# The block sums of G move from VectorE to GpSimd in a seven-product matrix multiplication

## The chip, the cores and the metric

The kernel runs on one core of a Trainium2 chip. The time is device microseconds of one execution; three runs of the kernel before are at hand. Five engines matter, each with its own instruction queue, executed in order: TensorE (PE in the profile, its weight loads PEld), VectorE (DVE), ScalarE (ACT), GpSimd (POOL) and the queue engine SP. Transfers between main memory and the on-chip memory (SBUF) are issued from a queue and carried by 16 DMA engines. TensorE writes to eight accumulator banks (PSUM).

## The reference

The kernel computes a weight gradient: the sum over all 16 x 512 = 8192 rows of the outer products of `input` (X, 1024 columns) and `grad_output` (G, 768 columns), in 32-bit floats.

```python
"input": np.random.randn(16, 512, 1024), "grad_output": np.random.randn(16, 512, 768)
grad_weight = np.einsum('bmk,bmn->kn', input, grad_output)   # 1024 x 768
```

## The kernel before, in words

**Tiles.** The 8192 rows are 32 units of 256 rows. A unit is one tile `xp` (128 partitions x 2 x 1024, bf16) and one tile `gp` (128 x 2 x 768, bf16); the transfer converts from 32 bits. `LOADS` names the kind of each unit: units 0 to 5 and 31 ("s") are multiplied in the ordinary way, units 6 to 30 ("P", 25 pairs) with seven block products in place of eight.

**The seven products.** For a pair, X and G are seen as 2 x 2 blocks: two halves of the rows by two halves of the columns (512 of X, 384 of G). `sum_x` forms three sums of blocks of X in three instructions, two of them into the tile `xe`, the last over a block of `xp` (stages x0, x1, x2); `sum_g` forms three of G into `ge` and, last, over a block of `gp` (stages g0, g1, g2). g0 adds two blocks at once (128 x 768), g1 adds a block to g0's result (128 x 384), g2 adds a block to g1's (128 x 384). The products are named by a letter or digit: A and 1 read raw blocks, B needs x2, C needs g2, 5 and 7 need x0 and g0, 6 needs x1 and g1 (`operands`, lines 224 to 243). Products are accumulated over many units, each in four strips of 128 columns of X (a name such as C2 is product C, strip 2).

**The plan.** The order on TensorE, VectorE and ScalarE is written out by hand in the list `PLAN`, and is executed as it stands. A token such as `C2.1` is one matmul of C2, `C2@2.2` is two into bank 2, newly opened; `fC3@6` fills bank 6 with an accumulated sum from SBUF (ScalarE), `v10` and `c10` close a bank into SBUF (VectorE or ScalarE), `x0.9` and `g2.9` are stages of the sums of unit 9. Around the last sum of G of pair 9 the plan reads:

```
60@6.3 cC1 61@2.1 g1.9 61.2 fB0@0 v60 10@5.2 c61 g2.9 B0.3 v10 fC3@6 C2@2.2 cB0 x0.9 C2.1
```

Sums come shortly before the products that read them: here `C2.1` is the first product to read g2 of pair 9. For pair 25 it is the first of `C2.3` in `50.4 vB2 B0@6.1 x0.25 f10@2 B0.3 c50 C2@5.1 x1.25 C2.3`.

**Transfers.** Unit 0's first half comes through SP and ScalarE. All other loads are issued by GpSimd, in order of the units, G ahead of X (lines 151 to 159): two issues for each unit from 2 on. An issue waits until the eighth issue before it has landed, that is, X of unit u+4 waits for X of unit u, and G of u+4 for G of u. Where a tile's buffer is used again (14 are held), it also waits for its last readers. Before the change nothing else stands on GpSimd's queue but four constants at the start. The results are stored by SP, the last also by ScalarE.

Of the kernel before, what the change touches and what calls it, by code (L numbers as in the profile page):

```python
# [9 lines left out]
P = 128  # L10

LOADS = "ssssssPPPPPPPPPPPPPPPPPPPPPPPPPs"
# [69 lines left out]
SUMS_HELD = 10  # L82

MERGED = 2


@with_exitstack
def kernel(
# [6 lines left out]
    nc = tc.nc  # L95
# [11 lines left out]
    X = input.rearrange("b m k -> (b m) k")  # L107
    G = grad_output.rearrange("b m n -> (b m) n")
# [35 lines left out]
    items = []  # L144
    tiles = {}
    for u, kind in enumerate(LOADS):
        pool = pairs if u else head
        xp = pool.tile([P, 2, K], bf16, name="xp", tag="xp")
        gp = pool.tile([P, 2, N], bf16, name="gp", tag="gp")
        if u >= MERGED:  # L150
            rows = slice(2 * u * P, 2 * (u + 1) * P)
            nc.gpsimd.dma_start(out=gp, in_=G[rows, :].rearrange("(p m) n -> p m n", m=2))  # L152
            nc.gpsimd.dma_start(out=xp, in_=X[rows, :].rearrange("(p m) k -> p m k", m=2))  # L153
        for h in range(2):
            s = 2 * u + h
            if s > 0 and u < MERGED:
                nc.gpsimd.dma_start(out=gp[:, h, :], in_=G[s * P : (s + 1) * P, :])
            if s > 1 and u < MERGED:
                nc.gpsimd.dma_start(out=xp[:, h, :], in_=X[s * P : (s + 1) * P, :])
            if kind == "s":  # L160
                items.append(("s", xp[:, h, :], gp[:, h, :]))
        tiles[u] = (xp, gp)
        if kind == "P":
            items.append(("P", u, None))

    extra = {}

    def sums_of(u):
        if u not in extra:
            extra[u] = (
                sums.tile([P, 3, KH], bf16, name="xe"),
                sums.tile([P, 3, NH], bf16, name="ge"),
            )
        return extra[u]
# [11 lines left out]
    def sum_g(stage, u):  # L189
        g = tiles[u][1].rearrange("p m (h n) -> p (m h) n", h=2)  # L190
        ge = sums_of(u)[1]
        if stage == 0:
            nc.vector.tensor_add(out=ge[:, 0:2, :], in0=g[:, 0:2, :], in1=g[:, 1::2, :])  # L193
        elif stage == 1:
            nc.vector.tensor_add(out=ge[:, 2, :], in0=g[:, 3, :], in1=ge[:, 0, :])  # L195
        else:
            nc.vector.tensor_add(out=g[:, 1, :], in0=ge[:, 2, :], in1=g[:, 2, :])  # L197

    def round_by(engine, dst, src, c0, c1):
        copy = nc.vector.tensor_copy if engine == "DVE" else nc.scalar.copy  # L200
# [129 lines left out]
    for token in PLAN:  # L330
        op, rest = token[0], token[1:]
        if op in "xg":
            stage, u = rest.split(".")
            (sum_x if op == "x" else sum_g)(int(stage), int(u))
        elif op == "r":
            round_by(*ROUNDINGS[int(rest)])
        elif op == "f":
            block, banks = rest.split("@")
            b, _, b2 = banks.partition("+")
            fill(block[0], int(block[1]), int(b), int(b2) if b2 else None)  # L340
        elif op in "cv":
            close(op, rest[0], int(rest[1]))
        else:
            block, n = token.split(".")
            block, _, b = block.partition("@")
            multiply(block[0], int(block[1]), int(b) if b else None, int(n))
# [32 lines left out]
```

## Time and profile before

| | |
|---|---|
| median of 3 runs | 162.96 us (162.92 to 163.28) |
| profiled execution, span from first to last instruction | 161.4 us; the median of the runs is 1.56 us longer |
| mean TensorE clock granted | 0.995 |
| matmuls | 937, from 0.8 to 157 us |
| VectorE busy | 143.0 us, of which sums of G 31.2, sums of X 38.0 |
| GpSimd busy | 34.6 us, nearly all of it 65 transfer issues |
| transfers from GpSimd | 60 of 384 or 512 KB, median 16.7 us from issue to landing |

The profile gives for the profiled execution only its span, no time of its own outside it. A row of a group reads: line, engine, operation, output <- inputs, shapes, count, then busy microseconds and mean nanoseconds of one, then the idle time of the engine just before. A row of the timeline reads: start, length, engine, line, operation, count. VectorE's and ScalarE's instructions overlap a little, so that the next starts some 0.08 us before the one before has ended.

### The profile page before, as it was taken

How to read it: one execution, taken by the hardware profiler on the slowest of the kernel's cores; microseconds unless marked ns; L12 is line 12 of the kernel's file. 1: busy time of each engine (PE TensorE's matmuls, PEld its weight loads, DVE VectorE, ACT ScalarE, POOL GpSimd, SP SyncE). 2: the span in 40 equal slices, each digit the busy share in tenths (PEclk: the TensorE clock that was granted, in tenths of full speed). 3: DMA queues.
4: the chain of work that ended last, by engine and by line, in shares of the span. 5: the costliest groups of instructions: out<-in, count | busy, mean ns of one | idle time of the engine just before them, and what ended most of it. 6: DMA issues, size and time to landing. Idle time of an engine off the chain costs nothing.

```text
span 161.4 us, 2771 instructions
## 1 busy us (share of the span) xinstructions
PE 156.2 (97%) x937; PEld 92.2 (57%) x937; DVE 143.0 (89%) x323; ACT 112.6 (70%) x253; POOL 34.6 (21%) x69
## 2 busy tenths in 40 slices
PE   8999999999999999999999999999999999999990
PEld 3355555666566665556665556665566665655560
DVE  0688986889999999999999998998899988989991
ACT  3679627749978999978878786525676278877630
POOL 7442221222221222222221222221222100000000
PEclk9999999999999999999999999999999999999998
DMA  5999999999999999999999999999999999905275
GB/s 168 297 211 213 211 216 212 212 214 211 215 211 215 213 211 213 213 212 214 210 214 214 216 213 213 211 212 211 212 212 213 213 213 213 202 18 195 107 283 195
DMA packets 12398, 33.40 MB, mean 207 GB/s; under 512 B 1376, under 2 KB 4192, under 8 KB 12384
## 3 DMA queue, kind: packets, MB, share of 16 engines
q0 software_dynamic: 9360, 28.64, 89.7%
q1 hardware_dynamic: 2592, 3.47, 6.2%
q10 hardware_dynamic: 432, 1.11, 1.9%
q8 instruction: 7, 0.11, 0.3%
q14 instruction: 7, 0.06, 0.1%
HBM read 58.72 MB, written 3.15 MB: 383 GB/s over the span
## 4 chain that ended last, share of the span: by engine, by line
PE 89%; DVE 4%; DMA 3%; issue 2%; ACT 1%; DVEq 0%; ACTq 0%
PE bank L286 89%; DMA xf<-in_input_dram 3%; DVE acc L310 2%; DVE macc L306 1%; DVEq L374 0%; DVE acc L325 0%; DVE macc L310 0%; DVE acc L323 0%; ACT bank L273 0%; ACT xp L201 0%; DVE macc L307 0%; DVEq L306 0%; ACTq L273 0%
## 5 line engine op out<-in xcount | busy, mean ns | idle before, releaser
L286 PE MATMUL bank<-gp,xp 128*128 128x384 bf16 (+2 forms) x631 | 110.2, 325 | 0.2
L286 PEld LDWEIGHTS <-xp 128*128 128x128 bf16 x631 | 61.4, 98 | 42.9 <-DVE xp L201 1.6
L286 PE MATMUL bank<-ge,xe 128*128 128x384 bf16 x300 | 56.2, 326 | 0.0
L273 ACT COPY bank<-macc 128x384 f32<-128x384 f32 x71 | 33.6, 484 | 13.0 <-DVE macc L325 5.5
L286 PEld LDWEIGHTS <-xe 128*128 128x128 bf16 x300 | 29.3, 98 | 19.5 <-issue 0.2
L273 ACT COPY bank<-acc 128x384 f32<-128x384 f32 (+1 forms) x70 | 32.3, 479 | 9.4 <-DVE acc L323 5.5
L321 ACT COPY macc<-bank 128x384 f32<-128x384 f32 x61 | 28.6, 479 | 9.4 <-PE bank L286 8.1
L325 DVE TENSOR_TENSOR acc<-bank,acc 128x384 f32<-128x384 f32 x54 | 28.7, 552 | 3.2 <-PE bank L286 1.6
L153 POOL DMA_DIRECT2D xp<-in_input_dram x30 | 15.9, 530 | 53.7 <-DMA xp<-in_input_dram 30.0
L321 ACT COPY acc<-bank 128x384 f32<-128x384 f32 x45 | 21.4, 480 | 7.3 <-PE bank L286 6.9
L152 POOL DMA_DIRECT2D gp<-in_grad_output_dram x30 | 15.9, 532 | 36.8 <-DMA gp<-in_grad_output_dram 14.4
L325 DVE TENSOR_TENSOR macc<-bank,macc 128x384 f32<-128x384 f32 x41 | 22.5, 551 | 0.5 <-PE bank L286 0.2
L183 DVE TENSOR_TENSOR xe<-xp 128x1024 bf16<-128x1024 bf16 x25 | 17.1, 682 | 0.3 <-DMA xp<-in_input_dram 0.3
L323 DVE COPY acc<-bank 128x384 f32<-128x384 f32 x24 | 13.1, 554 | 3.6 <-PE bank L286 3.0
L193 DVE TENSOR_TENSOR ge<-gp 128x768 bf16<-128x768 bf16 x25 | 13.7, 549 | 0.0
L187 DVE TENSOR_TENSOR xp<-xp,xe 128x512 bf16<-128x512 bf16 x25 | 10.5, 419 | 0.4
L185 DVE TENSOR_TENSOR xe<-xe,xp 128x512 bf16<-128x512 bf16 x25 | 10.4, 418 | 0.3
L197 DVE TENSOR_TENSOR gp<-ge,gp 128x384 bf16<-128x384 bf16 x25 | 8.8, 351 | 0.3
L195 DVE TENSOR_TENSOR ge<-gp,ge 128x384 bf16<-128x384 bf16 x25 | 8.7, 349 | 0.2
L310 DVE TENSOR_TENSOR acc<-bank,macc 128x384 f32<-128x384 f32 (+2 forms) x17 | 8.0, 523 | 0.0
L323 DVE COPY macc<-bank 128x384 f32<-128x384 f32 x14 | 7.6, 552 | 0.4 <-PE bank L286 0.4
L201 DVE CAST gp<-gf 128x192 bf16<-128x192 f32 (+1 forms) x2 | 0.7, 325 | 5.0 <-DMA gf<-in_grad_output_dram 5.0
(17 smaller groups left out, 22.2 us busy)
## 6 DMA issues: line engine op xcount, KB each, us to landing
xp<-in_input_dram POOLq DMA_DIRECT2D x30, 512.0 KB, 16.7
gp<-in_grad_output_dram POOLq DMA_DIRECT2D x30, 384.0 KB, 16.7
out_dram<-acc SPq DMA_DIRECT2D x15, 192.0 KB, 1.9
xf<-in_input_dram ACTq DMA_DIRECT2D x2, 512.0 KB, 5.0
gp<-in_grad_output_dram POOLq DMA_DIRECT2D x3, 192.0 KB, 6.7
xp<-in_input_dram POOLq DMA_DIRECT2D x2, 256.0 KB, 8.0
gf<-in_grad_output_dram SPq DMA_DIRECT2D x2, 192.0 KB, 4.2
out_dram<-acc SPq DMA_DIRECT2D x1, 128.0 KB, 2.0
```

Source lines behind the costliest of these rows:

```text
L152: nc.gpsimd.dma_start(out=gp, in_=G[rows, :].rearrange("(p m) n -> p m n", m=2))
L153: nc.gpsimd.dma_start(out=xp, in_=X[rows, :].rearrange("(p m) k -> p m k", m=2))
L183: nc.vector.tensor_sub(out=xe[:, 0:2, :], in0=x[:, 1::-1, :], in1=x[:, 3::-2, :])
L185: nc.vector.tensor_sub(out=xe[:, 2, :], in0=xe[:, 0, :], in1=x[:, 0, :])
L187: nc.vector.tensor_add(out=x[:, 1, :], in0=x[:, 2, :], in1=xe[:, 2, :])
L193: nc.vector.tensor_add(out=ge[:, 0:2, :], in0=g[:, 0:2, :], in1=g[:, 1::2, :])
L273: nc.scalar.copy(out=tile_[:, 0 : c1 - c0], in_=src[:, c0:c1])
L286: nc.tensor.matmul(tile_[:, 0 : c1 - c0], stat, mov[:, c0:c1], start=first and j == 0, stop=True, skip_group_check=True,)
L310: nc.vector.tensor_add(out=dst[:, c0:c1], in0=b, in1=sum_of(SHARED[p], q)[:, c0:c1])
L321: nc.scalar.copy(out=dst, in_=b)
L323: nc.vector.tensor_copy(out=dst, in_=b)
L325: nc.vector.tensor_add(out=dst, in0=b, in1=dst)
```

## The change

The three stages of `sum_g` are given to GpSimd, with the same operands. The loads are no longer all issued ahead of the plan: those up to unit 10 are (`AHEAD + LOADS.index("P")` is 10, the units 0 to 9, and stage 0 of unit 6 asks for unit 10), and from then on the loads of unit u+4 are issued right ahead of stage 0 of unit u. The plan itself isn't touched; its tokens `g0` to `g2` now stand on another queue.

In the changed program GpSimd's queue holds, for each pair u: the issue of G of unit u+4, the issue of X of unit u+4, g0, g1, g2 of unit u; g1 waits for g0 and g2 for g1 by a semaphore. The last four sums (27 to 30) have no issues between them. Ahead of the very first g0 stands one control instruction (`PseudoReloadLibraryIndex`, shown at line 203). VectorE has 75 instructions fewer.

```diff
@@ the loads @@
-        if u >= MERGED:
-            rows = slice(2 * u * P, 2 * (u + 1) * P)
-            nc.gpsimd.dma_start(out=gp, in_=G[rows, :].rearrange("(p m) n -> p m n", m=2))
-            nc.gpsimd.dma_start(out=xp, in_=X[rows, :].rearrange("(p m) k -> p m k", m=2))
...
+    issued = [0]
+
+    def issue_loads(upto):
+        while issued[0] < min(upto, len(LOADS)):
+            u = issued[0]
+            issued[0] += 1
+            xp, gp = tiles[u]
+            if u >= MERGED:
+                rows = slice(2 * u * P, 2 * (u + 1) * P)
+                nc.gpsimd.dma_start(out=gp, in_=G[rows, :].rearrange("(p m) n -> p m n", m=2))
+                nc.gpsimd.dma_start(out=xp, in_=X[rows, :].rearrange("(p m) k -> p m k", m=2))
+                continue
...
+    issue_loads(AHEAD + LOADS.index("P"))
@@ sum_g @@
         if stage == 0:
-            nc.vector.tensor_add(out=ge[:, 0:2, :], in0=g[:, 0:2, :], in1=g[:, 1::2, :])
+            issue_loads(u + 1 + AHEAD)
+            nc.gpsimd.tensor_add(out=ge[:, 0:2, :], in0=g[:, 0:2, :], in1=g[:, 1::2, :])
         elif stage == 1:
-            nc.vector.tensor_add(out=ge[:, 2, :], in0=g[:, 3, :], in1=ge[:, 0, :])
-        else:
-            nc.vector.tensor_add(out=g[:, 1, :], in0=ge[:, 2, :], in1=g[:, 2, :])
+            nc.gpsimd.tensor_add(out=ge[:, 2, :], in0=g[:, 3, :], in1=ge[:, 0, :])
+        else:
+            nc.gpsimd.tensor_add(out=g[:, 1, :], in0=ge[:, 2, :], in1=g[:, 2, :])
```

`AHEAD` is 4.

More of the change, by code (lines that the diff above doesn't have):

```diff
@@ L84 @@
 MERGED = 2
+AHEAD = 4
 @with_exitstack
@@ L149 @@
         gp = pool.tile([P, 2, N], bf16, name="gp", tag="gp")
-        if u >= MERGED:
-            rows = slice(2 * u * P, 2 * (u + 1) * P)
-            nc.gpsimd.dma_start(out=gp, in_=G[rows, :].rearrange("(p m) n -> p m n", m=2))
[L153 to L161, printed above, removed]
         tiles[u] = (xp, gp)
-        if kind == "P":
+        if kind == "s":
+            items += [("s", xp[:, h, :], gp[:, h, :]) for h in range(2)]
+        else:
             items.append(("P", u, None))
+    issued = [0]
[9 more added lines that the diff above has]
+                continue
+            for h in range(2):
+                at = slice((2 * u + h) * P, (2 * u + h + 1) * P)
+                if u or h:
+                    nc.gpsimd.dma_start(out=gp[:, h, :], in_=G[at, :])
+                if u:
+                    nc.gpsimd.dma_start(out=xp[:, h, :], in_=X[at, :])
+    issue_loads(AHEAD + LOADS.index("P"))
     extra = {}
```

## The prediction

> **What bounds the kernel now.** I read the page's busy times and slices first, then a window of the middle, the chain that ended last, the groups by line, and the timeline around single pairs.
>
> ```profile
> span 161.4 us, 2771 instructions
> PE 156.2 (97%) x937; PEld 92.2 (57%) x937; DVE 143.0 (89%) x323; ACT 112.6 (70%) x253; POOL 34.6 (21%) x69
> PEclk9999999999999999999999999999999999999998
> 20.00:140.00 120.00, 120.00 (x740) 72.22 (x739) 112.66 (x257) 87.93 (x199) 25.86 (x49) 1.00 1.07 213
> 17.61 132.31 PE bank L286 x812
> ```
>
> Lines four and five are a window (us, then busy PE, PEld, DVE, ACT, POOL, clock, DMA share, GB/s) and a piece of the chain. TensorE is busy 120.00 of 120 us at full clock, and the chain is matmuls alone from 17.6 to 149.9. So any time that a matmul waits in the middle is added to the end, and nothing taken off VectorE there can shorten it. POOL has time free: 25.86 of 120 us, all issues.
>
> ```profile
> L193 DVE TENSOR_TENSOR ge<-gp 128x768 bf16<-128x768 bf16 x25 | 13.7, 549 | 0.0
> L197 DVE TENSOR_TENSOR gp<-ge,gp 128x384 bf16<-128x384 bf16 x25 | 8.8, 351 | 0.3
> L195 DVE TENSOR_TENSOR ge<-gp,ge 128x384 bf16<-128x384 bf16 x25 | 8.7, 349 | 0.2
> L310 DVE TENSOR_TENSOR acc<-bank,macc 128x384 f32<-128x384 f32 x15 | 7.5, 547 | 0.0
> L310 DVE TENSOR_TENSOR acc<-bank,macc 128x128 f32<-128x128 f32 x1 | 0.3, 280 | 0.0
> L321 ACT COPY acc<-bank 128x384 f32<-128x384 f32 x45 | 21.4, 480 | 7.3 <-PE bank L286 6.9
> L273 ACT COPY bank<-acc 128x128 f32<-128x128 f32 x1 | 0.3, 263 | 0.0
> ```
>
> These are the prices: the three adds as they are now (0.55 + 0.35 + 0.35 = 1.25 us a pair), and two sizes each of a VectorE add and a ScalarE copy that take one element at a time, from which a rate follows.
>
> ```profile
> 34.83 0.53 POOL L153 DMA_DIRECT2D xp<-in_input_dram  x1 [1.92 <-DMA xp<-in_input_dram]
> 45.91 0.55 DVE L193 TENSOR_TENSOR ge<-gp 128x768 bf16<-128x768 bf16 x1
> 47.24 0.35 DVE L197 TENSOR_TENSOR gp<-ge,gp 128x384 bf16<-128x384 bf16 x1
> 46.94 3.25 PE L286 MATMUL bank<-gp,xp 128*128 128x384 bf16 x19
> 48.11 0.53 POOL L153 DMA_DIRECT2D xp<-in_input_dram  x1 [2.24 <-DVE macc L325]
> 115.74 0.36 DVE L197 TENSOR_TENSOR gp<-ge,gp 128x384 bf16<-128x384 bf16 x1
> 117.30 1.46 PE L286 MATMUL bank<-gp,xp 128*128 128x384 bf16 x8
> 117.08 0.53 POOL L153 DMA_DIRECT2D xp<-in_input_dram  x1 [1.88 <-DMA xp<-in_input_dram]
> ```
>
> The timeline (start, length). The issues of X for units 10, 13 and 29 stand at 34.83, 48.11 and 117.08. Each waits until the eighth issue before it has landed, here X of units 6, 9 and 25. From the first to the last are 19 pairs in 82.25 us: 4.33 us a pair is the transfers' pace. The last sum of pair 9 ends at 47.6. By the plan's order, after 1(0) x2, B0 x3 and C2 x2, the eighth matmul of the row at 46.94 is the first that reads it, at 46.94 + 7 x 0.1625 = 48.1 (20 us hold about 123 matmuls: 120.00 / 740). Pair 25's last sum ends at 116.1, and its reader, the sixth of the row at 117.30, starts at 118.1. The slack is 0.5 and 2.0 us.
>
> **The change, part by part.** The matmuls and their order stay; 75 adds go from VectorE's queue to POOL's.
>
> *Removed from VectorE:* 25 x 1.25 = 31 us of busy time. Worth 0: matmuls hide it, since none waits for an eviction in the middle (120.00 of 120). If sums come late, VectorE waits with TensorE and has this time to spare, so evictions add nothing either.
>
> *Place on POOL's queue:* the issues up to unit 10 come ahead of the first sum, in the order of before. From then on, the sums of pair u stand behind the issues of unit u+4, and the last of these waits for X of pair u to land, which the G sums themselves don't need. For pair 9: the issue starts at 48.11 and takes 0.53, so the adds start at 48.64, not at 45.91. Even at VectorE's speed they end at 49.9, where 48.1 is wanted: 1.8 us late.
>
> *The price of three adds on POOL* is shown by no row; POOL's only computing rows are constants one element wide (98 ns), which is a fixed part at most. Low end: VectorE's 1.25 us. For more: an engine that takes its two operands one after the other pays two passes. ScalarE's rate is (480 - 263) / 256 = 0.85 ns an element beside 0.155 us fixed; two passes over 768, 384 and 384 elements come to 1.46 + 0.81 + 0.81 = 3.07 us. VectorE's 32-bit rate, (547 - 280) / 256 = 1.04 ns beside 0.147, gives 3.65. High end: two passes at the slowest row, ScalarE's cast of 192 elements in 351 ns (1.83 ns each): 5.6 us. I take 3.4 us, between the two fitted rates, the rows nearest to an engine that streams. The Trainium skill, GPSIMD Engine Reference, Performance versus the Vector engine, has 4497 ns for an add of 2048 fp32 elements; scaled to 1536 that is an estimate of 3.4 us and would leave the sum where it is; no run here shows it yet.
>
> *POOL's period:* two issues of 0.53 and 3.4 make 4.46 us, above the transfers' 4.33. POOL becomes the slowest of the stages, and lateness grows by pair.
>
> *A control instruction* without a counterpart before stands ahead of the first add (line 203 of the changed kernel). No row has it: 0 at least; ScalarE's table load, 1.28 us, is the nearest of its kind and I take 1.3. It is paid once, and while POOL is the slowest, it stays in the end.
>
> *Added waits:* the second add waits for the first and the third for the second, now by POOL's semaphore (in the rate's uncertainty). Behind a waiting issue or add stand the next pair's issues. That starves no transfer: four pairs, 17 us of them, are under way, against at most some 5 us of adds. SP's and ScalarE's queues keep their order.
>
> *Contention:* VectorE keeps the three X sums of each pair, 0.68 + 0.42 + 0.42 = 1.52 us, which read two SBUF tensors as POOL's adds will. Whether the two engines can read at once is what no row shows: POOL reads no tile before, and X's first sum takes 679 to 691 ns whatever POOL issues. If not, they take turns, and POOL's period grows by what of the 1.52 does not fall under its 1.06 of issues: by 0.46 at least, 1.52 at most. So it is 4.92 to 5.98, middle 5.45. Nothing excludes that it is 0; I take the middle, since POOL would be reading 3.4 of 4.46 us, so a shared path would be met by nearly every X sum.
>
> *The sum:* the first add starts at 34.83 + 0.53 + 1.3 = 36.7. Pair 25's last add ends at 36.7 + 19 x 5.45 + 3.4 = 143.7, 25.6 us after 118.1. Pair 9's would be 8.4 late (36.7 + 3 x 5.45 + 3.4 = 56.5), so pair 25 decides. The span: 161.4 + 25.6 = 187.0. The runs' median is 162.96, 1.56 above the profiled span; the time is 188.6.
>
> The Trainium skill, SBUF — State Buffer, Who interferes with whom, says that a VectorE instruction with two SBUF inputs and a GpSimd instruction that reads SBUF exclude each other for a whole instruction. By that rule it is 188.6, and by the rows alone, where nothing slows down beside POOL, 169.7 (below). No trace here shows either yet.
>
> **Rivals.**
>
> *No turns.* Both engines read at once. Pair 25 ends at 36.7 + 19 x 4.46 + 3.4 = 124.8, 6.7 late: span 168.1, time 169.7. For it: no row shows interference. Against it: nothing in this trace either, the case doesn't occur. Its bounds are 166.6 (3.07 us: POOL keeps the transfers' pace, and pair 9 is late by 48.64 + 3.07 - 48.1 = 3.6) and 174.7 (3.65 us: 36.7 + 19 x 4.71 + 3.65 - 118.1 = 11.7).
>
> *Cheap adds.* POOL adds 16-bit data about as fast as VectorE. Then POOL keeps up, and only its place on the queue costs: 1.8 us at pair 9, some 2.3 with the control instruction, which delays the first pair. Time 164.8 to 165.3. Against it: POOL would have to add an element in 0.52 ns ((549 - 349) / 384, VectorE's 16-bit rate), against 0.85 to 1.04 for the engines above that take one element at a time, and without a second pass.
>
> *Not slower.* The sums of pair 9 come by 48.1 because the issue ahead of them lands its wait earlier. The trace gives X of pair 9 as landed by 48.0, since VectorE starts its first X sum at 48.01. It decides only if the adds run ahead of that issue, by 1.8 us at least. Then TensorE runs as before: 162.9, and at best some 0.6 less, the gaps between matmuls from 8.4 us on. Only a reordering of POOL's queue could bring it; the changed program's order shows the issue ahead.
>
> *The moves don't happen:* excluded, the changed program has 75 adds more on POOL and 75 fewer on VectorE.
>
> **How the numbers follow.** Turns: 0.50, 188.6, with 178.5 at 4.92 and 198.6 at 5.98 us a pair. No turns: 0.31, 169.7. Cheap adds: 0.15, 165. Not slower: 0.04. The range is 166 to 202: below it lie the not slower case and most of the cheap one; above it, adds of over 3.8 us with turns. The likeliest case alone: 177 to 202. Within 0.2% is about what a measurement of this kernel can't tell from no change: faster 0.02, same 0.02, slower 0.96.
>
> **What would show it.** Right: matmuls that wait for POOL; POOL busy at nearly 100% of the middle, 5 to 6 us a pair; adds of about 1.5 and 0.85 us; X sums that start late or show more than 691 ns; the DMA share under 1.07; the three G rows gone from VectorE. The control instruction: more than 0.6 us between 34.83 and the first add. Wrong: adds under 1 us in total per pair, POOL idle in the middle, X sums unchanged beside POOL's adds (no turns), or a clock under 1.0 from TensorE's new gaps, which I put at nothing.

## The result, and the profile after

The changed kernel takes 186.05 us (185.75 to 186.37, four runs) against 162.99 before: 1.1409 times as long, 95% interval 1.1394 to 1.1423. The profiled execution took 185.84 us, 183.6 of them its span. The prediction was 188.6, range 166 to 202. Two of the kernels below also had executions that ran longer at a lower granted clock; their times are given without those.

The page of the changed kernel: busy times, the clock in 40 slices, and the chain that ended last by engine; the last line is that chain before.

```profile
span 183.6 us, 2777 instructions
PE 163.1 (89%) x937; PEld 91.4 (50%) x937; DVE 158.4 (86%) x248; ACT 112.5 (61%) x253; POOL 131.8 (72%) x144
PEclk9999999978999999999999999999999999999998
DVE 46%; PE 22%; DMA 16%; issue 6%; POOL 4%; ACT 3%; DVEq 0%; POOLq 0%; ACTq 0%
PE 89%; DVE 4%; DMA 3%; issue 2%; ACT 1%; DVEq 0%; ACTq 0%
```

VectorE has 75 instructions fewer and is busy for 158.4 us instead of 143.0. The chain, 89% matmuls before, is now 46% VectorE, and GpSimd, where the moved work lies, has only 4% of it. The groups say why; the last three lines are the X sums before:

```profile
L203 POOL TENSOR_TENSOR ge<-gp 128x768 bf16<-128x768 bf16 x25 | 42.0, 1678 | 0.3
L205 POOL TENSOR_TENSOR ge<-gp,ge 128x384 bf16<-128x384 bf16 x25 | 30.9, 1236 | 2.0
L207 POOL TENSOR_TENSOR gp<-ge,gp 128x384 bf16<-128x384 bf16 x25 | 24.5, 980 | 2.0
L192 DVE TENSOR_TENSOR xe<-xp 128x1024 bf16<-128x1024 bf16 x25 | 39.3, 1573 | 0.0
L194 DVE TENSOR_TENSOR xe<-xe,xp 128x512 bf16<-128x512 bf16 x25 | 19.6, 783 | 0.3
L196 DVE TENSOR_TENSOR xp<-xp,xe 128x512 bf16<-128x512 bf16 x25 | 20.6, 823 | 0.4
L335 DVE TENSOR_TENSOR acc<-bank,acc 128x384 f32<-128x384 f32 x54 | 28.5, 550 | 6.7 <-PE bank L296 4.7
L183 DVE TENSOR_TENSOR xe<-xp 128x1024 bf16<-128x1024 bf16 x25 | 17.1, 682 | 0.3 <-DMA xp<-in_input_dram 0.3
L185 DVE TENSOR_TENSOR xe<-xe,xp 128x512 bf16<-128x512 bf16 x25 | 10.4, 418 | 0.3
L187 DVE TENSOR_TENSOR xp<-xp,xe 128x512 bf16<-128x512 bf16 x25 | 10.5, 419 | 0.4
```

The three adds take 3.89 us a pair on GpSimd. The three X sums, which stayed on VectorE with the same operands, went from 682, 418 and 419 ns to 1573, 783 and 823: 3.18 us a pair instead of 1.52. The evictions (line 335, one input from PSUM and one from SBUF) kept their length (550 ns, 552 before). A stretch of the two engines' timelines shows one pair:

```profile
59.98 1.66 POOL L203 TENSOR_TENSOR ge<-gp 128x768 bf16<-128x768 bf16 x1
61.72 1.25 POOL L205 TENSOR_TENSOR ge<-gp,ge 128x384 bf16<-128x384 bf16 x1
63.05 0.98 POOL L207 TENSOR_TENSOR gp<-ge,gp 128x384 bf16<-128x384 bf16 x1
65.08 1.66 POOL L203 TENSOR_TENSOR ge<-gp 128x768 bf16<-128x768 bf16 x1
60.76 1.44 DVE L192 TENSOR_TENSOR xe<-xp 128x1024 bf16<-128x1024 bf16 x1
62.59 0.66 DVE L194 TENSOR_TENSOR xe<-xe,xp 128x512 bf16<-128x512 bf16 x1
63.64 0.66 DVE L196 TENSOR_TENSOR xp<-xp,xe 128x512 bf16<-128x512 bf16 x1
```

The first X sum starts at 60.76, within GpSimd's first add, and ends at 62.20, 0.56 us after that add has ended at 61.64; alone it takes 0.68. GpSimd's second add, which starts meanwhile, takes 1.25 us. VectorE's second and third sum are each stretched in the same way, and end 0.28 us after GpSimd's second and third add. This repeats: of the 53 X sums that start between 55 and 145 us, all but one end 0.56 us (the first of a pair) or 0.28 us (the second and third) after the first, second or third add of GpSimd. So VectorE gets one X sum done for each add of GpSimd, and a pair of them takes as long as GpSimd takes for a pair: 5.10 us here (65.08 - 59.98), where the transfers' pace before was 4.33.

What TensorE waited for, in us, times and the longest:

```profile
PE bank L296 <- ACT bank L283: 5.3, 11, 1.3
PE bank L296 <- POOL gp L207: 3.8, 1, 3.8
PE bank L296 <- DVE xe L192: 1.5, 3, 0.8
```

It waited for GpSimd once, at pair 6 (35.4 to 39.2 us). From then on the waits lead to VectorE, and to ScalarE's fills, which wait for VectorE's evictions (by ScalarE's list, 16.1 us for the largest group, 6.6 before). By the plan's order and the timelines, each G sum from pair 7 on is ready 1.9 us or more ahead of its first reader, while eleven times a matmul starts within 0.1 us of the end of the X sum that it reads.

### The profile page after: what moved, and what is told of

Same layout as the page of the kernel before. It is cut to its first block, busy times and chain, and to the rows that moved or that the text cites. A ratio compares the mean times of both kernels' runs of the same rounds, so it can differ in the third digit from the quotient of the medians.

```text
span 183.6 us, 2777 instructions
## 1 busy us (share of the span) xinstructions
PE 163.1 (89%) x937; PEld 91.4 (50%) x937; DVE 158.4 (86%) x248; ACT 112.5 (61%) x253; POOL 131.8 (72%) x144
## 4 chain that ended last, share of the span: by engine, by line
DVE 46%; PE 22%; DMA 16%; issue 6%; POOL 4%; ACT 3%; DVEq 0%; POOLq 0%; ACTq 0%
PE bank L296 22%; DVE xe L192 16%; DMA xp<-in_input_dram 16%; DVE macc L335 8%; DVE xe L194 8%; DVE acc L335 5%; DVE xp L196 4%; ACT bank L283 3%; DVE macc L333 2%; DVE acc L320 2%; DVE acc L333 1%; ACT macc L331 1%; POOL gp L172 1%; POOL ge L203 1%; POOL ge L205 1%
## 5 line engine op out<-in xcount | busy, mean ns | idle before, releaser
L296 PE MATMUL bank<-gp,xp 128*128 128x384 bf16 (+2 forms) x631 | 113.5, 327 | 8.5 <-POOL gp L207 3.8
L296 PEld LDWEIGHTS <-xp 128*128 128x128 bf16 x631 | 61.6, 98 | 54.8 <-issue 12.3
L296 PE MATMUL bank<-ge,xe 128*128 128x384 bf16 x300 | 58.2, 326 | 7.0 <-ACT bank L283 3.5
L296 PEld LDWEIGHTS <-xe 128*128 128x128 bf16 x300 | 28.7, 97 | 30.5 <-issue 7.7
L203 POOL TENSOR_TENSOR ge<-gp 128x768 bf16<-128x768 bf16 x25 | 42.0, 1678 | 0.3
L192 DVE TENSOR_TENSOR xe<-xp 128x1024 bf16<-128x1024 bf16 x25 | 39.3, 1573 | 0.0
L205 POOL TENSOR_TENSOR ge<-gp,ge 128x384 bf16<-128x384 bf16 x25 | 30.9, 1236 | 2.0
L167 POOL DMA_DIRECT2D xp<-in_input_dram x30 | 16.1, 537 | 14.1 <-DMA xp<-in_input_dram 12.0
L207 POOL TENSOR_TENSOR gp<-ge,gp 128x384 bf16<-128x384 bf16 x25 | 24.5, 980 | 2.0
L335 DVE TENSOR_TENSOR macc<-bank,macc 128x384 f32<-128x384 f32 x41 | 22.1, 547 | 2.3 <-PE bank L296 2.1
L166 POOL DMA_DIRECT2D gp<-in_grad_output_dram x30 | 16.8, 561 | 7.4 <-DMA gp<-in_grad_output_dram 7.4
L196 DVE TENSOR_TENSOR xp<-xp,xe 128x512 bf16<-128x512 bf16 x25 | 20.6, 823 | 0.4
L194 DVE TENSOR_TENSOR xe<-xe,xp 128x512 bf16<-128x512 bf16 x25 | 19.6, 783 | 0.3
(17 smaller groups left out, 22.3 us busy)
```

What stands on the lines that cost most here:

```text
L192: nc.vector.tensor_sub(out=xe[:, 0:2, :], in0=x[:, 1::-1, :], in1=x[:, 3::-2, :])
L194: nc.vector.tensor_sub(out=xe[:, 2, :], in0=xe[:, 0, :], in1=x[:, 0, :])
L196: nc.vector.tensor_add(out=x[:, 1, :], in0=x[:, 2, :], in1=xe[:, 2, :])
L203: nc.gpsimd.tensor_add(out=ge[:, 0:2, :], in0=g[:, 0:2, :], in1=g[:, 1::2, :])
L205: nc.gpsimd.tensor_add(out=ge[:, 2, :], in0=g[:, 3, :], in1=ge[:, 0, :])
L207: nc.gpsimd.tensor_add(out=g[:, 1, :], in0=ge[:, 2, :], in1=g[:, 2, :])
```

## The experiments

The theory was that of the prediction: adds on GpSimd and two-input adds of VectorE take turns. Its rivals were that GpSimd's length and its place on the queue alone make the loss, and that any GpSimd work in SBUF hurts VectorE. All ratios are to the kernel before on the same chip. An edit is against the changed kernel where nothing else is said.

### Without the X sums

```diff
 def sum_x(stage, u):
+    sums_of(u)
+    return
...
-    "5": lambda: (xe[:, 0, k], ge[:, 0, :]),
+    "5": lambda: (x[:, 0, k], ge[:, 0, :]),
```

> The changed kernel without VectorE's three X sums of each pair (the products read raw blocks of X in their place, so that part of the computation is left out). Turns (an add on GpSimd and a VectorE add with two SBUF inputs exclude each other): GpSimd's second add falls from 1.25 to 0.91 us and the third from 0.97 to 0.91, its period from 5.10 to 4.83 us (1.66 + 0.91 + 0.91 + three gaps of 0.08 + 1.11 of issues). Pair 25's last sum ends at 35.2 + 19 x 4.83 + 3.6 = 130.6, 12.5 us after its use at 118.1: span 174, time 176. Rival, GpSimd's adds are that slow by themselves: second add stays at 1.25, period 5.1, time 180 or more.

172.99 us, ratio 1.061 (1.059 to 1.063). GpSimd's adds in this kernel:

```profile
L205 POOL TENSOR_TENSOR ge<-gp 128x768 bf16<-128x768 bf16 x25 | 41.4, 1655 | 0.3
L207 POOL TENSOR_TENSOR ge<-gp,ge 128x384 bf16<-128x384 bf16 x25 | 22.8, 911 | 2.0
L209 POOL TENSOR_TENSOR gp<-ge,gp 128x384 bf16<-128x384 bf16 x25 | 22.8, 910 | 2.0
```

3.48 us a pair is GpSimd's own price: (1655 - 911) / 384 = 1.94 ns an element beside 0.17 us fixed. Its period here is 4.68 us (67.82 - 63.14 between two first adds), so 0.42 of the 5.10 in the changed kernel comes from meeting X sums. Length and place alone cost 10.0 us; with the X sums it is 13.1 us more. These are not two shares that add up: the last experiment below loses as much as the changed kernel although nobody waits for GpSimd in it.

### Without the G sums at all

This edit is against the kernel before.

```diff
 def sum_g(stage, u):
+    sums_of(u)
+    return
...
-    "5": lambda: (xe[:, 0, k], ge[:, 0, :]),
+    "5": lambda: (xe[:, 0, k], g[:, 0, :]),
```

> The kernel before without the three G sums (the products read raw blocks of G, so that part of the computation is left out): VectorE gets the same 31 us back as by the change, and GpSimd gets nothing. By the prediction's first step, that is worth nothing, since TensorE has no gaps: 162.5 to 163.1. Rival, VectorE's load holds the kernel back somewhere: 161.5 or less.

162.99 us, ratio 1.0001 (0.9990 to 1.0012). Taking the 31 us off VectorE for nothing gains nothing.

### Loads issued behind the sums

```diff
         if stage == 0:
-            issue_loads(u + 1 + AHEAD)
             nc.gpsimd.tensor_add(...)
...
             nc.gpsimd.tensor_add(out=g[:, 1, :], ...)
+            issue_loads(u + 1 + AHEAD)
```

> The changed kernel with the loads of unit u+4 issued behind the three adds of pair u instead of ahead of them. Place on the queue matters: the first add starts when G of pair 6 has landed, at 32.2 in place of 35.2, TensorE's first wait of 4.1 us falls to about 1.2, and since GpSimd stays the slowest stage at 5.1 us a pair the whole gain of some 2.9 us is kept: 183.1. Rival, VectorE's stretched X sums set the pace and GpSimd's start does not: 185.5 to 186.5.

182.57 us, ratio 1.1195 (1.1175 to 1.1214): 3.5 us less than the changed kernel. The first add starts at 31.84 instead of 35.17, and the profile lists no wait of TensorE for GpSimd any more. So the place on the queue is worth 3.5 of the 23.1 us. But 182.57 without one direct wait for GpSimd's sums also says that their lateness is not what holds TensorE for the rest.

### The even pairs only

```diff
+        eng = nc.vector if u % 2 else nc.gpsimd
...
-            nc.gpsimd.tensor_add(...)
+            eng.tensor_add(...)
```

> The changed kernel with GpSimd doing the G sums of the even pairs only, VectorE those of the odd ones. GpSimd then needs about 6.1 us in two pairs of 4.33 and keeps up. Length alone (what costs is that GpSimd falls behind, and turns are hidden): only the place on the queue and the longer adds are left, some 5 us later against a slack of 1.0 at pair 22: 167. Turns: VectorE's X sums of every second pair are stretched by 1.66 us against 1.25 freed, and VectorE was 98% busy: 0.2 us a pair more, 170 or so.

178.73 us, ratio 1.0943 (1.0907 to 1.0978): more than either expectation. Half the adds on GpSimd cost two thirds of the whole change, with GpSimd idle in between (41.88 us busy of 60, against 58.02 in the changed kernel). That speaks against length alone, and says that meeting GpSimd's reads costs more than I had counted.

### Adds that nobody waits for, and fills

Here the G sums are on VectorE as before, and GpSimd does something useless at the place where the changed kernel has its adds.

```diff
+    made = accp.tile([P, N], bf16, name="made")
...
             issue_loads(u + 1 + AHEAD)
+            both = made.rearrange("p (h n) -> p h n", h=2)
+            nc.gpsimd.tensor_add(out=both, in0=g[:, 2:4, :], in1=g[:, 0::2, :])
+            nc.gpsimd.tensor_add(out=both[:, 0, :], in0=g[:, 3, :], in1=g[:, 0, :])
+            nc.gpsimd.tensor_add(out=both[:, 1, :], in0=g[:, 3, :], in1=g[:, 2, :])
-            nc.gpsimd.tensor_add(out=ge[:, 0:2, :], in0=g[:, 0:2, :], in1=g[:, 1::2, :])
+            nc.vector.tensor_add(out=ge[:, 0:2, :], in0=g[:, 0:2, :], in1=g[:, 1::2, :])
... # and so for the second and the third sum
```

> The kernel before, with the G sums on VectorE, and beside them on GpSimd three adds of the same sizes for each pair, at the place of the changed kernel, which read blocks of G and write to a tile that nobody reads. All lateness then comes from contention alone. Turns: VectorE, 98% busy before, has to fit six adds of two SBUF inputs a pair, 2.77 us, between GpSimd's: each waits up to a GpSimd add; period 6.5 to 7 us a pair, time 205 to 225. Rival, length alone (VectorE is not hurt beside GpSimd): 163 to 165.

224.2 and 225.4 us, some 61.6 more than before (163.24): at the upper end of what turns were expected to cost. The next kernel has fills in place of these adds:

```diff
+            for _ in range(5):
+                nc.gpsimd.memset(made, 1.0)
```

> As the run before, but GpSimd fills its tile with a constant five times for each pair (128x768 each) in place of the adds: it writes SBUF and reads nothing. Turns over reading: X and G sums on VectorE keep their 0.68, 0.42, 0.55 and 0.35 us, time 163 to 165. Rival, any GpSimd work in SBUF holds VectorE up: sums stretched as beside the adds, over 175.

167.26 us, ratio 1.025 (1.022 to 1.028), off both expectations. VectorE's sums keep their lengths (687, 421, 421, and 553, 352, 353 ns), but five fills and two issues are 4.93 us, longer than the transfers' pace, and loads come late. Four fills remove that:

> As the fills before, but four of 0.74 us instead of five, so that GpSimd's period is 4.2 us (four starts 0.78 apart and 1.07 of issues) and no longer above the transfers' 4.33. If the 4 us that five fills cost were late transfers only, it is 163 to 163.5 now. If writing beside VectorE costs something itself, it stays at 165 or more.

163.07 us, ratio 1.0013 (1.0003 to 1.0022). The fills and VectorE's first X sum:

```profile
L206 POOL MEMSET made<- 128x768 bf16 x100 | 74.2, 742 | 4.5
L192 DVE TENSOR_TENSOR xe<-xp 128x1024 bf16<-128x1024 bf16 x25 | 17.1, 683 | 0.2 <-DMA xp<-in_input_dram 0.2
```

GpSimd writes SBUF for 74 us here, and VectorE doesn't notice. With copies, one operand read, it is different again:

```diff
-            for _ in range(4):
-                nc.gpsimd.memset(made, 1.0)
+            both = made.rearrange("p (h n) -> p h n", h=2)
+            for _ in range(3):
+                nc.gpsimd.tensor_copy(out=both, in_=g[:, 2:4, :])
```

> As the four fills, but three copies on GpSimd (128x768, from a landed tile of G to the tile that nobody reads): one operand read, one written, while the G sums stay on VectorE. If what excludes VectorE's sums is any reading by GpSimd: VectorE's sums stretch, 180 to 220 as beside the idle adds. If it takes two operands: 163 to 163.5, the sums at their lengths of before.

195.6 us, ratio 1.199 (1.197 to 1.201), GpSimd less busy than with the fills:

```profile
L207 POOL COPY made<-gp 128x768 bf16<-128x768 bf16 x75 | 68.7, 916 | 3.3
L192 DVE TENSOR_TENSOR xe<-xp 128x1024 bf16<-128x1024 bf16 x25 | 22.3, 893 | 0.0
L208 DVE TENSOR_TENSOR ge<-gp 128x768 bf16<-128x768 bf16 x25 | 22.6, 905 | 0.0
```

So it is reading that collides, by one operand as by two. In these two kernels VectorE's six sums account for the loss. With the copies they take 0.893 + 0.643 + 0.608 + 0.905 + 0.470 + 0.645 = 4.16 us a pair instead of 2.77: 25 x 1.39 = 35 us, measured 32.6. With the adds they take 5.24 us: 25 x 2.47 = 62 us, measured 61.6. (With the adds the granted clock fell to a mean of 0.935, with the copies it was 0.999, so the copies are the cleaner of the two.)

### One of the three adds

```diff
-            nc.gpsimd.tensor_add(out=ge[:, 2, :], ...)
+            nc.vector.tensor_add(out=ge[:, 2, :], ...)
...
-            nc.gpsimd.tensor_add(out=g[:, 1, :], ...)
+            nc.vector.tensor_add(out=g[:, 1, :], ...)
```

> The changed kernel with only the first add (both blocks, 1.66 us) on GpSimd, the second and third on VectorE. GpSimd's period is 2.8 us, it keeps up by far. Length alone: only the place on the queue and 1.1 us more length, against the slack of 0.5 at pair 9: 166. Turns: GpSimd reads SBUF for 1.66 us of each pair, as much as in the mean of the half kernel, and VectorE's five adds of two inputs wait for it: 172 to 180.

189.51 us, ratio 1.1632 (1.1615 to 1.1649): with one add of three on GpSimd it is slower than with all of them, and slower than I expected by 10 us. GpSimd is idle for much of the time, yet VectorE has no time left (19.90 of 20 us busy from 60 to 80 and from 80 to 100). One add on GpSimd and two of VectorE's sums:

```profile
87.34 1.65 POOL L203 TENSOR_TENSOR ge<-gp 128x768 bf16<-128x768 bf16 x1
91.65 1.65 POOL L203 TENSOR_TENSOR ge<-gp 128x768 bf16<-128x768 bf16 x1
87.22 1.99 DVE L205 TENSOR_TENSOR ge<-gp,ge 128x384 bf16<-128x384 bf16 x1
91.41 2.19 DVE L194 TENSOR_TENSOR xe<-xe,xp 128x512 bf16<-128x512 bf16 x1
```

A sum of 0.35 us takes 1.99, one of 0.42 takes 2.19. Each ends 0.2 to 0.3 us after GpSimd's add does (88.99 and 93.30), though by the trace it had started 0.12 and 0.24 us ahead of it. VectorE still has five sums of two inputs a pair here, and what it has queued behind a stopped sum, evictions above all, stops with it. That this is why one add costs more than three was not tested.

The third add alone, the first two given back to VectorE:

```diff
-            nc.gpsimd.tensor_add(out=ge[:, 0:2, :], ...)
+            nc.vector.tensor_add(out=ge[:, 0:2, :], ...)
...
-            nc.gpsimd.tensor_add(out=ge[:, 2, :], ...)
+            nc.vector.tensor_add(out=ge[:, 2, :], ...)
```

> The changed kernel with only the third add (0.91 us) on GpSimd. Length alone: the issue of X of unit u+4 still stands ahead, so pair 9's last sum ends at 48.64 + 0.91 = 49.6 where 48.1 is wanted: 164.5. Turns: GpSimd reads for 0.91 us a pair, about half of the first add's, so about half of its loss: 166 to 171.

164.42 us, ratio 1.0090 (1.0075 to 1.0105). The row of the timeline at pair 9:

```profile
49.53 1.79 PE L296 MATMUL bank<-gp,xp 128*128 128x384 bf16 x10 [0.40 <-POOL gp L207]
```

The 25 short adds meet few of VectorE's sums (X sums of 871, 440 and 418 ns), so the place on the queue is left. Issuing the loads behind the add takes that away:

```diff
         if stage == 0:
-            issue_loads(u + 1 + AHEAD)
...
             nc.gpsimd.tensor_add(out=g[:, 1, :], ...)
+            issue_loads(u + 1 + AHEAD)
```

> Only the third add on GpSimd, and the loads issued behind it instead of ahead. If the 1.5 us that the third add alone cost were its place behind the issue (and not VectorE's X sums meeting it), they go: 162.7 to 163.3, and nothing is gained by the 9 us taken off VectorE. Turns as the cause of the 1.5 us: it stays at 164 or more, as the add now falls elsewhere among VectorE's sums.

163.14 us, ratio 1.0003 (0.9993 to 1.0012). The place was all of it, and moving a third of the instructions for free gains nothing. The first X sum still takes 821 ns here instead of 682, and that costs nothing.

### VectorE's share, with nobody waiting for GpSimd

The kernel with the useless adds again, now without any G sums: VectorE has the work it has in the changed kernel, meets the same adds, and no product needs them.

```diff
     # GpSimd's three useless adds as above, then:
-            nc.vector.tensor_add(out=ge[:, 0:2, :], ...)
...
-    "5": lambda: (xe[:, 0, k], ge[:, 0, :]),
+    "5": lambda: (xe[:, 0, k], g[:, 0, :]),
```

> The kernel with the three adds on GpSimd writing to a tile that nobody reads, and no G sums at all (the products read raw blocks of G, so that part is left out). VectorE carries what it does in the changed kernel and meets the same adds; no one waits for GpSimd's results. If the changed kernel's end is set by the lateness of GpSimd's sums: 163 to 168 (transfers a little late at a period of 5.1). If it is set as much by VectorE, whose X sums wait for GpSimd's adds: 180 to 186.

185.7 us (185.5 to 185.9), ratio 1.1402 (1.1383 to 1.1421), the changed kernel's 1.1409 within that interval. The changed kernel loses nothing more when the products must also wait for GpSimd. Its end is set by VectorE's X sums, which GpSimd's reads hold up.

## Why the prediction was right, and where it was not

**TensorE has no gaps, so relief of VectorE is worth nothing.** Right: 162.99 without G sums, 163.14 with a third moved for free. The rival of no loss could only have come from the queue's order, and with that order mended, for the third add alone, it is a ratio of 1.0003, no gain.

**The place on the queue.** Right as a mechanism. For the third add alone, the prediction's working for pair 9 (ends at 49.6, wanted at 48.1) gave 1.5 us, and 1.5 were measured; in the changed kernel it is 3.5, and the wait stands at pair 6 (3.8 us), where the prediction had looked at pairs 9 and 25 only.

**The price of the adds.** 3.4 us was taken, 3.48 measured without X sums beside. The two-pass rows of 32-bit work were a good guide to the size (3.07 and 3.65); that GpSimd makes two passes is not shown. The estimate of 3.4 that the prediction made from the Trainium skill, GPSIMD Engine Reference, Performance versus the Vector engine, agrees with the 3.48.

**The control instruction.** 1.3 us was taken from ScalarE's table load; it appears twice with 37 ns, and the first add starts 0.1 us after the issue ahead of it has ended. The term was 1.2 too large.

**Turns.** Right as a mechanism: without X sums GpSimd's second add falls from 1.24 to 0.91 us, without GpSimd's reads the X sums fall from 3.18 to 1.52 us a pair. Fills left the first X sum at 683 ns, copies and adds stretched it, and the evictions with one SBUF input kept 550 ns beside the adds. The Trainium skill, SBUF — State Buffer, Who interferes with whom, says that a VectorE instruction with two SBUF inputs contends with a GpSimd instruction that reads SBUF and not with one that only writes it, and that one with a single SBUF input does not contend (outside what it calls 2-port perf modes). This case's runs agree on all three.

**Who pays for the turns.** This step failed. The prediction put them on GpSimd's period, 0.46 to 1.52 us and 0.99 taken. GpSimd's adds grew by 0.41 us a pair, and VectorE's X sums by 1.66. The prediction had written that VectorE "has this time to spare", so it let pair 25's last G sum decide. In the changed kernel that sum ends at 135.6, 17.5 us later than its use before (118.1), but the last matmul is 22.1 later (179.1 after 157.0): its lateness explains 17.5 at most. The run in which nobody waits for G sums takes 185.7 all the same. Pair 25's reader runs 2.6 us after the sum, and TensorE waits for GpSimd once in the whole trace. What the prediction lacked is the price of a stopped instruction on a full in-order queue: VectorE was busy for 112.66 of 120 us (94%) before, and became 1.25 us a pair lighter and 1.66 heavier. GpSimd's period did set the pace, but by another way than the prediction's: through the X sums, one of which got done for each add, and not through late G sums.

**The total.** 188.6 against 186.05 is close because errors cancel, and that is luck. Pair 25's last G sum was put at 143.7 and ends at 135.6, 8 us earlier: the first add starts at 35.2 in place of 36.7 (1.5 us, most of it the control instruction), the 19 periods up to pair 25 take 5.06 on average in place of 5.45 (7.3 us), and pair 25's own adds take 0.9 longer. Against this stand the 4.7 us by which the end (22.2 us later in span) exceeds the lateness of that sum. In span it was 187.0 against 183.6.

**What stays open.** The VectorE sums' growth accounts for the loss where all sums are on VectorE (35 us for 32.6, 62 for 61.6). In the changed kernel 25 x (1.66 - 1.25) is only 10 of 23 us, and the step into which the X sums fell says more. The first X sum of pair 9 ends at 57.1, 8.4 us later than before (48.7), and that of pair 26 at 144.0, 22.3 later (121.7). Over these 17 pairs VectorE went at 5.11 us a pair, as GpSimd's first adds did, in place of 4.30. That is read from the traces; no run changed the length of GpSimd's adds to test it. Nor was it tried whether X sums on another engine would end it.

## What to carry to other kernels

Before work is moved to an idle engine, ask what the busy one does at the same time: GpSimd's reads of SBUF stop VectorE's adds of two SBUF tensors, and a full in-order queue passes each stop on to everything behind it. Test that with work nobody waits for: it took one run here, and gave the whole loss. And where TensorE has no gaps, relief of another engine buys nothing: 31 us taken off VectorE changed nothing here.

## What the runs showed of the hardware that was not expected

- The two engines don't share the loss. In the changed kernel GpSimd's adds grew by 0.41 us a pair, VectorE's X sums by 1.66; a VectorE sum recorded as starting 0.24 us ahead of a GpSimd add still ended 0.30 after it. Starts on GpSimd are rough in the profile, so whether the later one takes over, or its reads begin ahead of its recorded start, stays open.
- A copy on GpSimd, one operand read, stops VectorE as an add does: 163 to 195.6 us, where fills of similar busy time (74.2 us against 68.7) cost 0.2.
- After TensorE's wait of 3.8 us (35.4 to 39.2), the granted clock is 0.50 for 3.2 us. Two windows of the changed kernel (us, then busy PE, PEld, DVE, ACT, POOL, clock, DMA share, GB/s):

```profile
35.10:39.20 4.10, 0.33 (x3) 0.10 (x1) 4.03 (x3) 0.37 (x1) 3.87 (x4) 0.99 1.06 210
39.20:42.40 3.20, 3.16 (x11) 1.48 (x11) 0.27 (x1) 1.62 (x4) 3.11 (x4) 0.50 1.06 212
```

A wait of 1.7 us at that place (the first add alone, 35.8 to 37.5) did not bring it, one of 3.2 us (without the X sums, to 38.7) did. The prediction had put a drop of the clock at nothing, and it hardly mattered in the end: the four executions lie between 183.2 and 184.0 us of span, the one at full clock at 183.2.
